# FFN entry and modulation loads: chains apart, own buffers, the factor between token halves, GpSimd's additions on VectorE

## The chip, the cores and the metric

The kernel runs on one core of a Trainium2 chip. The metric is the device time in microseconds of one execution, the median of three runs. TensorE (PE in the profile, with PEld for its weight loads), VectorE (DVE), ScalarE (ACT), GpSimd (POOL) and SyncE (SP, which issues the DMA of weights) work side by side, each through its own queue in order, and wait for each other by semaphores.

## The reference, cut to what matters

Two transformer blocks, each of two layers, run one after the other on 512 tokens of width 1024; the first block has 256 context tokens as well in its first layer.

```python
# first block, per layer: a modulation of six vectors from c (and from c_ctx)
mod_l = split(silu(c) @ ada_w[layer] + ada_b[layer], 6)
h_lat = rms(xl) * (1 + mod_l[1]) + mod_l[0]
y_lat = mixer(h_lat, ...)            # layer 0: conv + mLSTM scans; layer 1: latent attention (MLA)
xl = xl + mod_l[2] * y_lat
xl = xl + mod_l[5] * conv_ffn(rms(xl) * (1 + mod_l[4]) + mod_l[3])   # 1024 -> 2 x 2816 -> 1024
# second block, per layer
m = hybrid_mixer(rms_norm(x))        # differential attention, three dilated windows, rotary embedding
x = x + rms_norm(m)
x = x + rms_norm(swiglu(rms_norm(x)))
```

All is float32. The 12 MB matrix `ada_w[0]` is read for layer 0, and as much for layer 1.

## The kernel before, in words

Activations lie with the 1024 channels on partitions, in eight tiles (k = 0 to 7) of 128 channels by 512 tokens (768 with the context). A float32 product is made of three matmuls: each operand is split into a high part that the fast matmul format holds and a low remainder, and `staged`, `fm_g` and the helpers around line 366 issue high by high, high by low and low by high for each k. `weights` (L282) loads 512 KB of a weight matrix by SP's queue into a tile `raw`, ScalarE casts it to `whi` (L287), VectorE subtracts for `wlo` (L288). The pool `w` holds three buffers of each of the three tags.

The program runs through `first` (norm and first modulation), `mixer0` (convolution and mLSTM, 62 to 385 us, with its output projection to about 445 us), `conv_ffn` of layer 0 (to 1047 us), `mixer1a` and `mixer1b` (MLA, to 1450 us), `conv_ffn` of layer 1 (to 1835 us), then for each layer of the second block `mixer2` and `ffn2` (1835 to 2770 us, 2770 to 3746 us).

An FFN begins with `staged`: the weights of its first three column blocks stand ready, and three chains of 8 x 3 matmuls run over the eight k, k outermost, so that each new tile of the normed input (`h`, or `xg` in the second block) feeds three chains. In the FFNs with context that is done for the context, then for the latent tokens; elsewhere for the two halves of the tokens (`HALF`, 256 each). The normed input comes tile by tile from a loop on VectorE and ScalarE (`turn_loop`, `post_loop` with `pre_g`), and the sums of squares from `add_sq` (L460) and `pre_g` (L1487), with GpSimd adding the squares that ScalarE makes. The rms factor itself is made by `rstd` and `make_R`: TensorE sums over partitions (L434, L438), VectorE scales (L446), GpSimd takes the power -1/2 (L448, `rs_x`), TensorE broadcasts (L454). In the second block the factor R isn't applied to `xg` but to the products behind it, so it is wanted only with the first products; `mixer2` and `ffn2` call `make_R` before the first group of `staged`.

The modulation matrices are read by `ada` (L523): a generator that loads 512 KB through `raw`, so through the same three buffers as the weight matrices, and issues two matmul rows per load on a PSUM tile `ps_ad` (L536). It is drawn on by `side` and `fill` as side work amid the mLSTM (`more`), at the turn and in `conv_ffn` (two loads after each pair of hidden blocks). `rope` (L1533, second block) makes the rotary embedding: ScalarE copies the product out of PSUM, four DMAs swap halves (`rsw`), VectorE multiplies by the cosine (L1540), GpSimd by the sine (L1541), VectorE adds (L1546 or L1548).

The code gives what depends on what; a scheduler with its own estimates of durations sets the order on each engine from it, within the buffers of the pools. `pin` ties some instructions to a place relative to TensorE's work.

Of the kernel before, what the change touches and what calls it, by code (L numbers as in the profile page):

```python
# [14 lines left out]
AF = mybir.ActivationFunctionType  # L15
# [217 lines left out]
class Prog:  # L233
# [225 lines left out]
    def add_sq(self, S, k, src, a, tile):  # L459

        nc = self.nc
        n = src.shape[-1]
        q = S[0][:, a : a + n]
        if k == 0:
            nc.scalar.activation(q, src, AF.Square)
            return
        t = tile()[:, :n]
        nc.scalar.activation(t, src, AF.Square)  # L468
        if k < KD - 1:
            self.pin(nc.gpsimd.tensor_tensor(q, q, t, ALU.add))  # L470
        else:
            S[1] = t
# [53 lines left out]
    def ada(self, layer, ch):  # L526
# [137 lines left out]
    def staged(self, srcs, rhs, ctx=False, tag="mm"):  # L664

        mm = self.mm
        ws = [self.weights(s, lo=self.nc.vector) for s in srcs]

        def chains(ws, outs, a, b):
            for k in range(KD):  # L670
                xh, xl = (t[:, a:b] for t in rhs[k])
                for (wh, wl), o in zip(ws, outs):
                    w = slice(P * k, P * k + P)
                    mm(o, wh[:, w], xh, start=(k == 0), stop=False)
                    mm(o, wh[:, w], xl, start=False, stop=False)
# [12 lines left out]
        chains(ws, lat, TC, TA)  # L688
        return [list(q) for q in zip(lat, c)]
# [376 lines left out]
    def conv_ffn(self, layer, hs, ctx, begin, sq, loop=None):  # L1066
# [6 lines left out]
        with tc.tile_pool(name=f"f{layer}", bufs=1) as fp:  # L1073
# [7 lines left out]
            first = self.staged([up[i] for i in range(3)], hs, ctx)  # L1081
# [85 lines left out]
    def mixer1a(self, mp, hs):  # L1167
        nc, tc, I = self.nc, self.tc, self.I
        SEG = self.SEG
        if True:  # L1170
# [4 lines left out]
            with tc.tile_pool(name="m1t", bufs=2) as tp:  # L1175
# [6 lines left out]
                nc.gpsimd.tensor_tensor(acc, acc, s, ALU.add)  # L1182
# [37 lines left out]
                for k in range(4):  # L1220
# [3 lines left out]
                    else:  # L1224
                        s = self.tl(tp, [P, TA], "sqt")
                        nc.scalar.activation(s[:, :T], o, AF.Square)
                        if k < 3:
                            nc.gpsimd.tensor_tensor(acc[:, :T], acc[:, :T], s[:, :T], ALU.add)
# [101 lines left out]
    def mla_kv(self, tp, qd, ckv, rc, KR, krs, Ks, Vs):  # L1330
        nc = self.nc
        w = self.weights(self.I["m_ukv"][qd])
        for tb in range(6):
# [14 lines left out]
            nc.gpsimd.tensor_tensor(k[:, :, 0:64], k[:, :, 0:64], rk.unsqueeze(2).to_broadcast([P, 4, 64]), ALU.mult)  # L1348
            nc.gpsimd.tensor_tensor(
# [7 lines left out]
    def mla_q(self, tp, qd, cq, rq, tab, Qs, scs):  # L1357
        nc = self.nc
        ws = [self.weights(self.I["m_uq"][qd * 2 + i], 768) for i in range(2)]
        for tb in range(4):  # L1360
# [17 lines left out]
            for i, src in enumerate((r1, r2, r1, r2)):  # L1378
                nc.gpsimd.tensor_tensor(t[:, i], src, tab[:, i, tb].unsqueeze(1).to_broadcast([P, 4, 16]), ALU.mult)
# [110 lines left out]
    def pre_g(self, st, k, a, b):  # L1490
# [4 lines left out]
        if k == 0:  # L1495
            nc.scalar.activation(acc[:, a:b], x, AF.Square)
        else:
            s = sq()
            nc.scalar.activation(s[:, : b - a], x, AF.Square)
            self.pin(nc.gpsimd.tensor_tensor(acc[:, a:b], acc[:, a:b], s[:, : b - a], ALU.add))  # L1500
        return low

    def post_loop(self, ys, R, g, a, b, after):
# [3 lines left out]
        after_last = int(g == "ffn_post1")  # L1507
# [11 lines left out]
    XP = ((), (0, 2, 4, 6))  # L1519
# [10 lines left out]
    def rope(self, ap, ps, classes=False):  # L1530
# [10 lines left out]
        nc.gpsimd.tensor_tensor(sw, sw, self.SR, ALU.mult)  # L1541
# [11 lines left out]
    def mixer2(self, l, xg, acc, after):  # L1553
        nc, tc, I = self.nc, self.tc, self.I
        av = acc.rearrange("p (i b) -> p i b", b=4)
        R = self.make_R(acc)
        for k in range(KD):
            for t in xg[k]:
                tc.keep_in_program_order(nc.gpsimd.tensor_copy(t[:, T:TX], t[:, :64]))
        r = self.rstd(  # L1560
            [acc[:, i * P : i * P + P] for i in range(4)] + [av[:, :, b] for b in range(4)]
            + [[(0, acc[:, 448:]), (64, acc[:, :64])]] + [acc[:, t : t + P] for t in V0[1:]], D, EPS, "x12",
        )
        with tc.tile_pool(name=f"ma{l}", bufs=2) as ap:
            tab = ap.tile([P, 2, T], F32, name="rope2", bufs=1)
            nc.sync.dma_start(tab, I["rope2"])
            nc.vector.tensor_tensor(tab, tab, R.unsqueeze(1).to_broadcast([P, 2, T]), ALU.mult)
# [45 lines left out]
            for i, (o,) in enumerate(self.staged(srcs[:3], xg)):  # L1613
                dq[i // 2].append(rope(o))
# [80 lines left out]
    def merge(self, ap, l, gates, gts, of):  # L1695
# [10 lines left out]
        for d in range(KD):  # L1706
# [5 lines left out]
            nc.gpsimd.tensor_tensor(g[0], g[0], g[1], ALU.add)  # L1712
# [224 lines left out]
    def ffn2(self, l, xg, acc, nxt, after):  # L1937
        nc, tc, I = self.nc, self.tc, self.I
        R = self.make_R(acc)
        with tc.tile_pool(name=f"sf{l}", bufs=1) as fp, tc.tile_pool(name=f"st{l}", bufs=2) as tp:  # L1940
            ys = [fp.tile([P, T], F32, name=f"fy{k}") for k in range(KD)]
            acc, acc2 = (self.tl(tp, [P, T], "nacc", bufs=2) for _ in range(2))
            S = [acc, None]
# [37 lines left out]
            first = [o for (o,) in self.staged([I[f"sup{l}"][i] for i in range(3)], xg)]  # L1981
# [154 lines left out]
```

## Time and profile before

| | us |
|---|---|
| median of three runs | 3740.7 (3739.66 to 3743.14) |
| the profiled execution | 3747.83, span 3746.0 |
| TensorE busy in the span | 3625.1 (97%) |
| VectorE, ScalarE, GpSimd busy | 2154.5, 1417.7, 412.7 |
| TensorE's mean granted clock | 0.985 |

The clock is given as a share of full speed, 2.4 GHz; its other level is 0.5. Busy times are of the one profiled execution, and a row of the profile always names the line of the kernel that issued the instruction. Matmuls overlap each other, so the distance between two starts, and not the length of one, is what a matmul costs in a dense stretch.

### The profile page before, as it was taken

Reading aid. Unit: us, or ns where it says so; the run is one execution under the profiler, and the core shown is the slowest. Engines: PE = TensorE matmul, PEld = TensorE weight load, DVE = VectorE, ACT = ScalarE, POOL = GpSimd, SP = SyncE. Lnnn points to the kernel's source line nnn. Section 1 sums busy time; section 2 is a strip of 40 time slices with the busy share of each in tenths; the row PEclk is TensorE's granted clock in tenths of the full one; section 3 lists DMA queues with packets and bytes.
Section 4 is the critical chain, followed back from the end, with each engine's and each line's share of the span. In section 5 each row is a group of like instructions: output and inputs, shape, how many; then the busy total and the mean of one; then the engine's idle time right before and its main releaser. Section 6 shows DMA issues by size and latency. Waiting matters only on the chain. (4 is left out here: it accounts for less than half of the span.)

```text
span 3746.0 us, 50182 instructions
## 1 busy us (share of the span) xinstructions
PE 3625.1 (97%) x19870; PEld 2980.6 (80%) x19870; DVE 2154.5 (58%) x3568; ACT 1417.7 (38%) x2540; POOL 412.7 (11%) x460
## 2 busy tenths in 40 slices
PE   8999999999989999999999999999999999999998
PEld 5767777888876767888887888888888887888887
DVE  6958454444447676555575655645567655555545
ACT  3246232222236555333353333432235433333222
POOL 0000100000024211000201110300031111020001
PEclk9999999999999999999999999999999999999999
DMA  5242223331111011232333322233324333222332
GB/s 211 78 159 87 72 89 124 114 107 63 58 51 30 27 35 53 93 96 96 99 111 96 100 87 79 82 93 101 96 80 123 103 91 91 74 85 90 96 100 75
DMA packets 107387, 336.89 MB, mean 90 GB/s; under 512 B 14864, under 2 KB 19600, under 8 KB 106896
## 3 DMA queue, kind: packets, MB, share of 16 engines
q1 hardware_dynamic: 94864, 316.89, 26.6%
q10 hardware_dynamic: 12288, 16.79, 1.7%
q8 instruction: 156, 2.56, 0.3%
q14 instruction: 79, 0.65, 0.1%
HBM read 310.55 MB, written 2.10 MB: 83 GB/s over the span
## 5 line engine op out<-in xcount | busy, mean ns | idle before, releaser
L287 ACT CAST whi<-raw 128x1024 fp32r<-128x1024 f32 (+2 forms) x487 | 501.1, 1031 | 1201.1 <-PE ps_mm L367 764.7
L288 DVE TENSOR_TENSOR wlo<-raw,whi 128x1024 fp32r<-128x1024 f32 (+2 forms) x487 | 614.5, 1263 | 372.3 <-ACT whi L287 369.9
L367 PE MATMUL ps_mm<-h,whi 128*128 128x512 f32 (+1 forms) x2561 | 638.4, 356 | 7.7 <-DVE fy L1136 3.4
L367 PE MATMUL ps_mm<-xg,whi 128*128 128x512 f32 (+1 forms) x1865 | 554.5, 379 | 9.7 <-DVE xg L302 6.7
L367 PEld LDWEIGHTS ps_mm<-h,whi 128*128 128x128 f32 x2561 | 424.4, 189 | 94.9 <-issue 14.0
L367 PE MATMUL ps_mm<-hid,whi 128*128 128x512 f32 (+1 forms) x1805 | 469.3, 357 | 0.0
L367 PEld LDWEIGHTS ps_mm<-xg,whi 128*128 128x128 f32 x1865 | 346.5, 190 | 78.3 <-DVE xg L302 11.1
L366 PE MATMUL ps_mm<-xg,whi 128*128 128x512 f32 (+1 forms) x1271 | 390.3, 387 | 2.7 <-DVE xg L302 2.7
L367 PE MATMUL ps_mm<-h,wlo 128*128 128x512 f32 (+1 forms) x1282 | 391.3, 354 | 0.5 <-DVE wlo L288 0.5
L367 PEld LDWEIGHTS ps_mm<-hid,whi 128*128 128x128 f32 x1805 | 310.2, 188 | 59.5 <-issue 6.7
L367 PE MATMUL ps_mm<-xg,wlo 128*128 128x512 f32 (+1 forms) x934 | 350.7, 378 | 0.5 <-DVE wlo L288 0.5
L367 PE MATMUL ps_mm<-hid,wlo 128*128 128x512 f32 (+1 forms) x903 | 299.2, 356 | 0.0
L366 PEld LDWEIGHTS ps_mm<-xg,whi 128*128 128x128 f32 x1271 | 233.4, 190 | 48.7 <-DVE xg L302 4.3
L367 PEld LDWEIGHTS ps_mm<-h,wlo 128*128 128x128 f32 x1282 | 216.2, 190 | 37.2 <-DVE wlo L288 1.0
L366 PE MATMUL ps_mm<-xg,wlo 128*128 128x512 f32 (+1 forms) x634 | 240.6, 382 | 0.0
L367 PEld LDWEIGHTS ps_mm<-xg,wlo 128*128 128x128 f32 x934 | 177.7, 190 | 32.6 <-DVE wlo L288 1.0
L367 PEld LDWEIGHTS ps_mm<-hid,wlo 128*128 128x128 f32 x903 | 160.3, 188 | 24.9
L1541 POOL TENSOR_TENSOR rsw<-rsw,rope 128x512 f32<-128x512 f32 x64 | 109.6, 1714 | 465.4 <-DMA rsw<-rsw 285.7
L366 PEld LDWEIGHTS ps_mm<-xg,wlo 128*128 128x128 f32 x634 | 120.0, 189 | 23.0
L1160 DVE SCALAR_TENSOR_TENSOR xl<-ps_mm,mod,xl 128x512 f32<-128x512 f32 (+1 forms) x102 | 73.0, 717 | 109.4 <-PE ps_mm L367 108.7
L366 PE MATMUL ps_mm<-whi,xg 128*128 128x512 f32 x384 | 131.7, 411 | 1.9 <-ACT qk L1535 1.9
L829 DVE SCALAR_TENSOR_TENSOR acc<-up,cw,acc 128x783 f32<-128x783 f32 x120 | 120.6, 1027 | 1.2
(569 smaller groups left out, 5665.3 us busy)
## 6 DMA issues: line engine op xcount, KB each, us to landing
raw<-in_fup SPq DMA_DIRECT2D x88, 512.0 KB, 3.5
raw<-in_sup SPq DMA_DIRECT2D x88, 512.0 KB, 3.5
raw<-in_ada SPq DMA_DIRECT2D x80, 512.0 KB, 3.8
raw<-in_l_qk SPq DMA_DIRECT2D x48, 512.0 KB, 3.6
raw<-in_fdn SPq DMA_DIRECT2D x32, 512.0 KB, 3.5
raw<-in_d_v SPq DMA_DIRECT2D x32, 512.0 KB, 3.7
raw<-in_d_gt SPq DMA_DIRECT2D x32, 512.0 KB, 3.6
raw<-in_sdn SPq DMA_DIRECT2D x32, 512.0 KB, 3.4
```

The costliest lines, as they stand in the source:

```text
L287: self.nc.scalar.copy(h[:, :n], r[:, :n])
L288: (lo or self.nc.vector).tensor_tensor(l[:, :n], r[:, :n], h[:, :n].bitcast(F32), ALU.subtract)
L366: return self.nc.tensor.matmul(out, w, x, **k)
L367: return self.nc.tensor.matmul(out, w, x, **k)
L829: nc.vector.scalar_tensor_tensor(acc, u, s, acc, ALU.mult, ALU.add)
L1160: self.pin(nc.vector.scalar_tensor_tensor(xs, o[:, : b - a], self.m(layer, 5, d, int(a < TC)), xs, ALU.mult, ALU.add))
L1541: nc.gpsimd.tensor_tensor(sw, sw, self.SR, ALU.mult)
```

## The change

Five edits, each in several places:

1. `ada` loads into tiles `adaw` of its own, two buffers in the pool `ad`, instead of `raw`.
2. `staged` takes `apart`: for the last three k the loop goes chain by chain, not k by k. `conv_ffn` and `ffn2` call it with 3.
3. `staged` takes `between`, a function called between the two token halves; `mixer2` and `ffn2` make the prenorm factor there.
4. In `add_sq` and `pre_g` the addition of squares goes from GpSimd to VectorE and is issued one k later, so that VectorE doesn't wait for ScalarE's square.
5. Other elementwise operations go from GpSimd to VectorE: residual additions of the last post loop, the multiplications in `rope`, K, Q and norms of the MLA mixer, one gate sum in `mixer2`.

```diff
@@ add_sq
-        if k < KD - 1:
-            self.pin(nc.gpsimd.tensor_tensor(q, q, t, ALU.add))
-        else:
+        for u, v in S[2:]:
+            self.pin(nc.vector.tensor_tensor(u, u, v, ALU.add))
+        S[2:] = [(q, t)] if k < KD - 1 else []
+        if k == KD - 1:
             S[1] = t
@@ ada
-                r = self.raw(self.I[f"ada{layer}"][(ch + c if layer else ch + c - 4) * 4 + kg])
+                r = self.tl(self.adp, [P, WC], "adaw", bufs=2)
+                nc.sync.dma_start(r, self.I[f"ada{layer}"][(ch + c if layer else ch + c - 4) * 4 + kg])
@@ staged
-    def staged(self, srcs, rhs, ctx=False, tag="mm"):
+    def staged(self, srcs, rhs, ctx=False, tag="mm", apart=0, between=None):
...
         def chains(ws, outs, a, b):
-            for k in range(KD):
+            pairs = list(zip(ws, outs))
+            n = KD - apart
+            order = [(k, i) for k in range(n) for i in range(len(pairs))]
+            order += [(k, i) for i in range(len(pairs)) for k in range(n, KD)]
+            for k, i in order:
+                (wh, wl), o = pairs[i]
                 xh, xl = (t[:, a:b] for t in rhs[k])
-                for (wh, wl), o in zip(ws, outs):
-                    w = slice(P * k, P * k + P)
-                    mm(o, wh[:, w], xh, start=(k == 0), stop=False)
-                    mm(o, wh[:, w], xl, start=False, stop=False)
-                    mm(o, wl[:, w], xh, start=False, stop=(k == KD - 1))
+                w = slice(P * k, P * k + P)
+                mm(o, wh[:, w], xh, start=(k == 0), stop=False)
+                mm(o, wh[:, w], xl, start=False, stop=False)
+                mm(o, wl[:, w], xh, start=False, stop=(k == KD - 1))
...
             for a, b in self.HALF:
                 chains(ws, [o[:, a:b] for o in outs], a, b)
+                if between and a == 0:
+                    between()
@@ conv_ffn
-            first = self.staged([up[i] for i in range(3)], hs, ctx)
+            first = self.staged([up[i] for i in range(3)], hs, ctx, apart=3)
@@ pre_g
-        else:
-            s = sq()
-            nc.scalar.activation(s[:, : b - a], x, AF.Square)
-            self.pin(nc.gpsimd.tensor_tensor(acc[:, a:b], acc[:, a:b], s[:, : b - a], ALU.add))
-        return low
+            return low
+        s = sq()[:, : b - a]
+        nc.scalar.activation(s, x, AF.Square)
+
+        def rest():
+            self.pin(low())
+            return nc.vector.tensor_tensor(acc[:, a:b], acc[:, a:b], s, ALU.add)
+
+        return rest
@@ post_loop
-            self.pin((nc.gpsimd if k in self.XP[after_last] else nc.vector).tensor_tensor(x, x, y, ALU.add))
+            self.pin(nc.vector.tensor_tensor(x, x, y, ALU.add))
@@ rope
-        nc.gpsimd.tensor_tensor(sw, sw, self.SR, ALU.mult)
+        nc.vector.tensor_tensor(sw, sw, self.SR, ALU.mult)
@@ mixer2 (ffn2 likewise, with make_R alone and apart=3)
-        R = self.make_R(acc)
+        R = r = None
...
+            def factors():
+                nonlocal R, r
+                R = self.make_R(acc)
+                nc.vector.tensor_tensor(tab, tab, R.unsqueeze(1).to_broadcast([P, 2, T]), ALU.mult)
+                r = self.rstd(...)
...
-            for i, (o,) in enumerate(self.staged(srcs[:3], xg)):
+            for i, (o,) in enumerate(self.staged(srcs[:3], xg, between=factors)):
```

The same replacement of `nc.gpsimd` by `nc.vector` is made in `mixer1a`, `mixer1b`, the K and Q parts of MLA and the gate sum of `mixer2`.

How the orders differ at three places. On TensorE in the mLSTM's steps behind the second head: `xl` and `xc` are the scores' operands, `v,S` the products with the values, `cmu` and `g_T` belong to the convolution's norm. Before:

```order
L1039 MATMUL ps_ml_2591<-v_4_1673,S_414_2607 128x129
L1039 MATMUL ps_ml_2591<-v_5_1676,S_414_2607 128x129
L1003 MATMUL ps_ml_2680<-xl_915,xc_1262 128x128 x2
L1003 MATMUL ps_ml_2680<-xl_915,xl_1261 128x128 x2
L454 MATMUL ps_st_2508<-con,cmu_2506 128x128 x4
L454 MATMUL ps_st_2509<-con,cmu_2506 128x128 x2
L1003 MATMUL ps_ml_2681<-xl_915,xl_1261 128x128 x2
L1039 MATMUL ps_ml_2680<-v_0_1661,S_431_2688 128x129
L1039 MATMUL ps_ml_2680<-v_1_1664,S_431_2688 128x129
```

and now:

```order
L1047 MATMUL ps_ml_2591<-v_5_1676,S_414_2607 128x129
L1011 MATMUL ps_ml_2680<-xl_915,xc_1262 128x128 x2
L454 MATMUL ps_st_2508<-con,cmu_2506 128x128 x4
L454 MATMUL ps_st_2509<-con,cmu_2506 128x128 x2
L1011 MATMUL ps_ml_2680<-xl_915,xl_1261 128x128 x2
L1011 MATMUL ps_ml_2681<-xl_915,xl_1261 128x128 x2
L538 MATMUL ps_ad_2707<-adaw_4479,sc 32x512 x2
L538 MATMUL ps_ad_2707<-adaw_4483,sc 32x512 x2
L454 MATMUL ps_st_2641<-con_593,g_T_696 128x128 x4
L548 MATMUL ps_ad_4489<-con,adarow_4487 128x8 x4
L454 MATMUL ps_st_2642<-con_593,g_T_696 128x128 x2
```

The matmuls of two modulation loads (`adaw`) stand now between the scores and the convolution's norm, where before there was none in such a step.

On TensorE at the first group of the conv FFN of layer 0, `ps_mm_3956`, `3957` and `3958` are the three chains, `4135` the fourth, which takes the PSUM buffer that the first pair's work leaves free. Before, the end of the three chains:

```order
L367 MATMUL ps_mm_3956<-h_3315,whi_3938 128x512
L367 MATMUL ps_mm_3956<-h_3316,whi_3938 128x512
L367 MATMUL ps_mm_3956<-h_3315,wlo_3939 128x512
L367 MATMUL ps_mm_3957<-h_3315,whi_3944 128x512
L367 MATMUL ps_mm_3957<-h_3316,whi_3944 128x512
L367 MATMUL ps_mm_3957<-h_3315,wlo_3945 128x512
L367 MATMUL ps_mm_3958<-h_3315,whi_3950 128x512
L367 MATMUL ps_mm_3958<-h_3316,whi_3950 128x512
L367 MATMUL ps_mm_3958<-h_3315,wlo_3951 128x512
L367 MATMUL ps_mm_4135<-h_3301,whi_4131 128x512
```

and now:

```order
L367 MATMUL ps_mm_3958<-h_3314,whi_3950 128x512
L367 MATMUL ps_mm_3958<-h_3313,wlo_3951 128x512
L367 MATMUL ps_mm_3958<-h_3315,whi_3950 128x512
L367 MATMUL ps_mm_3958<-h_3316,whi_3950 128x512
L367 MATMUL ps_mm_3958<-h_3315,wlo_3951 128x512
L538 MATMUL ps_ad_5555<-adaw_6390,sc 32x512 x2
L538 MATMUL ps_ad_5555<-adaw_6456,sc 32x512 x2
L367 MATMUL ps_mm_4135<-h_3301,whi_4131 128x512
```

The last nine matmuls of each chain stand together now (of the third the last five are shown), and the matmuls of two modulation loads stand ahead of the fourth chain.

On VectorE in the differential attention of the second block, `p` are the probabilities, `drs` their factors, `rope` the tables. Before:

```order
L1846 TENSOR_SCALAR p_16091<-p_16091,drs_16093 128x512
L1540 TENSOR_TENSOR qk_16134<-qk_16134,rope_15374 128x512
L1847 SCALAR_TENSOR_TENSOR p_16086<-p_16086,drs_16093,p_16091 128x512
L288 TENSOR_TENSOR wlo_16325<-raw_16322,whi_16324 128x1024
L1838 TENSOR_REDUCE mx_16184<-ps_st_16178 128x1
L446 TENSOR_SCALAR rv_d_2971_16172<-dss_15809 128x4
L1548 TENSOR_TENSOR qk_16134<-qk_16134,rsw_16136 128x512
```

and now, in such a unit:

```order
L1861 TENSOR_SCALAR p_16621<-p_16621,drs_16623 128x512
L1550 TENSOR_TENSOR rsw_16691<-rsw_16691,rope_15340 128x512
L1551 TENSOR_TENSOR rsw_16693<-rsw_16693,rope_15340 128x512
L1862 SCALAR_TENSOR_TENSOR p_16616<-p_16616,drs_16623,p_16621 128x512
L1556 TENSOR_TENSOR qk_16690<-rsw_16691,rsw_16693 128x512
```

The multiplication by the sine (L1551) stands in VectorE's queue, where it stood in GpSimd's.

## Rows read from the trace of the kernel before

**Rows 1.** page, busy time of each engine, share of the span, number of instructions

```profile
PE 3625.1 (97%) x19870; PEld 2980.6 (80%) x19870; DVE 2154.5 (58%) x3568; ACT 1417.7 (38%) x2540; POOL 412.7 (11%) x460
```

**Rows 2.** stretches: length, then PE, PEld, DVE, ACT, POOL busy (x), PEclk, DMA share, GB/s

```profile
319.00:361.00 42.00, 36.55 (x245) 32.87 (x244) 35.60 (x100) 32.32 (x100) 2.64 (x2) 0.88 0.08 23
...
443.00:460.00 17.00, 12.30 (x77) 9.47 (x78) 4.84 (x10) 2.32 (x5) 1.74 (x2) 0.80 0.45 147
479.00:490.00 11.00, 7.64 (x27) 5.86 (x26) 9.71 (x13) 6.51 (x9) 0.00 (x0) 0.84 0.47 143
490.00:1047.00 557.00, 554.18 (x3183) 465.46 (x3181) 259.52 (x366) 154.61 (x193) 13.66 (x12) 1.00 0.29 92
```

**Rows 3.** two of the stretches, line L536 (modulation matmuls) alone: PE, PEld, PEclk, DMA share, GB/s

```profile
319.00:361.00 42.00, 0.00 (x0) 0.00 (x0) 0.88 0.08 23
490.00:1047.00 557.00, 23.96 (x144) 3.66 (x144) 1.00 0.29 92
```

**Rows 4.** waits of PE: engine, tile, line <- releaser: us in total, times, longest us

```profile
PE ps_st L1854 <- DVE p L1847: 7.7, 4, 3.0
...
PE ps_ad L536 <- DMA raw<-in_ada: 6.9, 5, 3.9
PE ps_mm L367 <- DVE xg L302: 6.7, 19, 1.6
PE ps_st L454 <- POOL rs_x L448: 5.7, 5, 1.4
...
PE ps_st L434 <- POOL p L470: 1.6, 1, 1.6
...
PE ps_st L434 <- POOL GB L470: 1.4, 1, 1.4
```

**Rows 5.** groups by line and shape, GpSimd: xcount | busy us, mean ns | idle

```profile
L1541 POOL TENSOR_TENSOR rsw<-rsw,rope 128x512 f32<-128x512 f32 x64 | 109.6, 1714 | 465.4 <-DMA rsw<-rsw 285.7 <-DMA rsw<-qk 147.9 <-PE ps_mm L367 14.7
```

**Rows 6.** page, DMA issues: xcount, KB each, median us from issue to landing

```profile
raw<-in_ada SPq DMA_DIRECT2D x80, 512.0 KB, 3.8
```

**Rows 7.** timeline at the turn: start us, us, engine, line, tiles, count, idle before

```profile
442.41 0.80 SPq L279 DMA_DIRECT2D raw<-in_ada  x2
...
448.08 3.19 PE L536 MATMUL ps_ad<-raw,sc 128*32 128x512 f32 x8 [3.92 <-DMA raw<-in_ada]
```

**Rows 8.** timeline at the conv FFN's first pair

```profile
473.98 0.39 PE L367 MATMUL ps_mm<-h,wlo 128*128 128x512 f32 x1
...
474.20 0.62 PE L367 MATMUL ps_mm<-h,whi 128*128 128x512 f32 x2
...
482.28 0.74 DVE L1136 SCALAR_TENSOR_TENSOR fy<-ps_mm,par,fy 128x511 f32<-128x511 f32 x1
...
483.17 0.70 PE L367 MATMUL ps_mm<-h,whi 128*128 128x512 f32 x2 [3.36 <-DVE fy L1136]
```

**Rows 9.** timeline in the post loop at an entry, VectorE and GpSimd

```profile
2409.40 0.48 DVE L302 SCALAR_TENSOR_TENSOR xg<-xl,par,xg 128x256 fp32r<-128x256 f32 x1
...
2410.30 0.42 DVE L1511 TENSOR_TENSOR xl<-xl,v 128x256 f32<-128x256 f32 x1
...
2410.41 0.91 POOL L1500 TENSOR_TENSOR rsw<-rsw,p 128x256 f32<-128x256 f32 x1 [2.06 <-ACT p L1499]
...
2410.65 0.96 DVE L302 SCALAR_TENSOR_TENSOR xg<-xl,par,xg 128x256 fp32r<-128x256 f32 x1
```

**Rows 10.** timeline in the differential attention, VectorE and GpSimd

```profile
2019.67 0.49 DVE L1846 TENSOR_SCALAR p<-p,drs 128x512 f32<-128x512 f32 x1
...
2033.16 0.69 DVE L1540 TENSOR_TENSOR rsw<-rsw,rope 128x512 f32<-128x512 f32 x1 [0.89 <-DMA rsw<-rsw]
2033.29 1.68 POOL L1541 TENSOR_TENSOR rsw<-rsw,rope 128x512 f32<-128x512 f32 x1 [6.38 <-DMA rsw<-rsw]
2033.77 1.49 DVE L1846 TENSOR_SCALAR p<-p,drs 128x512 f32<-128x512 f32 x1
...
2036.57 1.11 PE L1854 MATMUL ps_st<-con,p 128*128 128x128 f32 x4 [2.99 <-DVE p L1847]
```

More of the change, by code (lines that the diff above doesn't have):

```diff
@@ L1181, in mixer1a @@
                         self.split(ckv[k][0][:, a:b], ckv[k][1][:, a:b], o[:, : b - a], scale=self.par("kv_norm", k, k + 1))
-                nc.gpsimd.tensor_tensor(acc, acc, s, ALU.add)
+                nc.vector.tensor_tensor(acc, acc, s, ALU.add)
                 rc = self.rstd([acc[:, i * P : i * P + P] for i in range(6)], 256, EPS, "rc")
@@ L1227, in mixer1a @@
                         if k < 3:
-                            nc.gpsimd.tensor_tensor(acc[:, :T], acc[:, :T], s[:, :T], ALU.add)
+                            nc.vector.tensor_tensor(acc[:, :T], acc[:, :T], s[:, :T], ALU.add)
                     self.split(cq[k][0], cq[k][1], o, scale=self.par("q_norm", k, k + 1))
@@ L1347, in mla_kv @@
             rk = self.rstd_of(ss, 4, 96, EPS, "k4")
-            nc.gpsimd.tensor_tensor(k[:, :, 0:64], k[:, :, 0:64], rk.unsqueeze(2).to_broadcast([P, 4, 64]), ALU.mult)
-            nc.gpsimd.tensor_tensor(
+            nc.vector.tensor_tensor(k[:, :, 0:64], k[:, :, 0:64], rk.unsqueeze(2).to_broadcast([P, 4, 64]), ALU.mult)
+            nc.vector.tensor_tensor(
                 k[:, :, 64:96], KR[:, tb].unsqueeze(1).to_broadcast([P, 4, 32]),
@@ L1378, in mla_q @@
             for i, src in enumerate((r1, r2, r1, r2)):
-                nc.gpsimd.tensor_tensor(t[:, i], src, tab[:, i, tb].unsqueeze(1).to_broadcast([P, 4, 16]), ALU.mult)
+                nc.vector.tensor_tensor(t[:, i], src, tab[:, i, tb].unsqueeze(1).to_broadcast([P, 4, 16]), ALU.mult)
             nc.vector.tensor_tensor(r1, t[:, 0], t[:, 1], ALU.subtract)
@@ L1517, in post_loop @@
             self.pin(low())
-    XP = ((), (0, 2, 4, 6))
     def make_R(self, acc):
@@ L1559, in mixer2 @@
                 tc.keep_in_program_order(nc.gpsimd.tensor_copy(t[:, T:TX], t[:, :64]))
[L1560 to L1563, printed above, removed]
         with tc.tile_pool(name=f"ma{l}", bufs=2) as ap:
@@ L1566, in mixer2 @@
             nc.sync.dma_start(tab, I["rope2"])
-            nc.vector.tensor_tensor(tab, tab, R.unsqueeze(1).to_broadcast([P, 2, T]), ALU.mult)
+            def factors():
+                nonlocal R, r
+                R = self.make_R(acc)
+                nc.vector.tensor_tensor(tab, tab, R.unsqueeze(1).to_broadcast([P, 2, T]), ALU.mult)
+                r = self.rstd(
+                    [acc[:, i * P : i * P + P] for i in range(4)] + [av[:, :, b] for b in range(4)]
+                    + [[(0, acc[:, 448:]), (64, acc[:, :64])]] + [acc[:, t : t + P] for t in V0[1:]], D, EPS, "x12",
+                )
             self.CR, self.SR = tab[:, 0], tab[:, 1]
@@ L1711, in merge @@
                 nc.vector.scalar_tensor_tensor(g[i], g[i], 1.0, q, ALU.add, ALU.mult)
-            nc.gpsimd.tensor_tensor(g[0], g[0], g[1], ALU.add)
+            nc.vector.tensor_tensor(g[0], g[0], g[1], ALU.add)
             hl = [self.tl(ap, [P, T], "od", F32R, bufs=4) if d < 4 else rest[:, d - 4], lows[d // 4][:, d % 4]]
@@ L1938, in ffn2, with factors @@
         nc, tc, I = self.nc, self.tc, self.I
-        R = self.make_R(acc)
+        R = None
         with tc.tile_pool(name=f"sf{l}", bufs=1) as fp, tc.tile_pool(name=f"st{l}", bufs=2) as tp:
             ys = [fp.tile([P, T], F32, name=f"fy{k}") for k in range(KD)]
-            acc, acc2 = (self.tl(tp, [P, T], "nacc", bufs=2) for _ in range(2))
-            S = [acc, None]
+            sums, acc2 = (self.tl(tp, [P, T], "nacc", bufs=2) for _ in range(2))
+            S = [sums, None]
+            def factors():
+                nonlocal R
+                R = self.make_R(acc)
             def hidden(g, u):
@@ L1980, in ffn2 @@
             pend = None
-            first = [o for (o,) in self.staged([I[f"sup{l}"][i] for i in range(3)], xg)]
+            first = [o for (o,) in self.staged([I[f"sup{l}"][i] for i in range(3)], xg, apart=3, between=factors)]
             first.append(up(3))
```

1 line of the change is left out of this document (removed).

## The prediction

> **What bounds the kernel now.** First the page's busy times: TensorE is busy for 97% of the span, VectorE for 58%, ScalarE for 38%, GpSimd for 11% [rows 1]. So the time is TensorE's own work plus the moments in which it stands or runs at the lower clock, and an edit on another engine counts only where it ends such a moment. Work that is moved from one place of TensorE's queue to another is not saved; it is saved only as far as it falls into idle time there.
>
> Next the table of stretches, which says where that idle time is [rows 2]. In the first conv FFN (490 to 1047 us) TensorE is busy for 554.18 of 557 us at full clock: whatever leaves that stretch shortens it one to one. In the last part of the mLSTM (319 to 361 us) it is busy for 36.55 of 42 us, and the granted clock is 0.88 in the mean, a mixture of 2.4 GHz and 1.2 GHz: 5.45 us idle and, at 12% of 42 us, some 5.0 us lost to the clock, together about 10.5 us that other work could fill. At the turn from the mixer to the FFN (443 to 460 us) 4.7 of 17 us are idle and the clock is 0.80; at the FFN's first pair (479 to 490 us) 3.36 of 11 us, at 0.84.
>
> Then the waits of TensorE, which name who ends them [rows 4]: the modulation weights' DMA (6.9 us in five waits), VectorE's prenorm chunks (6.7 us in 19), the attention's p (7.7 us in four), GpSimd's rs_x (5.7 us in five), and GpSimd's sums of squares at the turns (1.6 and 1.4 us). Together under one percent of the span; this is the field on which the change plays, and no edit of it can bring much more than 1%.
>
> **Own buffers for the modulation weights.** There are 80 loads of 512 KB, each used by two matmul rows. Before, they take turns with the weight matrices in three buffers; now they have two of their own, and nothing but their own use holds them back. In the order the loads then stand earlier. Counted by place (before the mLSTM; mLSTM up to 319 us; its rest; turn; conv FFN) there were 11, 29, 0, 4 and 36; now there are 19, 25, 22.5, 10.5 and 3 (a half is a load whose two rows are apart). The price of one: the 36 loads in the conv FFN are 144 records of 23.96 us [rows 3], so 0.67 us each.
>
> The sum by places. Out of the dense conv FFN go 33 x 0.67 = 22.0 us, in full. Eight more before the mLSTM, where TensorE is dense too, cost 5.3 us; four fewer up to 319 us give 2.7 us; 6.5 more at the turn cost 4.3 us. That is +6.9 us. Left are 22.5 loads in the 42 us from 319 us on, where there were none [rows 3]: 15.0 us of work. If everything idle there is filled, the stretch grows by 15.0 - 10.5 = 4.5 us, and the whole edit gives -22.0 + 6.9 + 4.5 = -10.6 us. But with two buffers a load can be issued only when the load before the last has been used, so two loads pass in one landing plus one use. The median landing is 3.8 us [rows 6], so the pace is (3.8 + 0.67) / 2 = 2.2 us a load, 22.5 x 2.2 = 50 us, a growth of 8 us. So the edit gives **-7 us**. The far end is the landing of a crowded moment: two loads issued together at 442.41 us were awaited until 448.08 us, 5.6 us [rows 7]. At that landing the pace is 3.1 us, the stretch 70.5 us, and the edit +13.4 us. It is even where the stretch becomes 57 us, at a landing of 4.4 us. I take the median since little else is loaded from 319 us on: the DMA share there is 0.08 [rows 2].
>
> The Trainium skill ("Trainium Kernel Development and Optimization", Best Practices) advises to double-buffer so that DMA and compute overlap. By that alone the 22.5 loads would cost no wait and the edit would be at its -10.6 us; the rows of the trace allow it only if a landing is below the time between two uses, which here is about the same.
>
> At the turn itself the wait of 3.92 us for the DMA [rows 7] doesn't simply go: five loads now stand there in a row, of which two buffers can hold two. The others are issued as the first are used, and land after the FFN's first h chunks are ready anyway. I take 0, between -3.9 and +4 (one more such wait).
>
> **The last three h tiles chain by chain.** In the conv FFN's first group three chains of 24 matmuls ran abreast, and the first ended six matmuls before the last. Now its end comes 18 matmuls before the last one's, 12 earlier. These matmuls start 0.23 us apart (473.98, 474.20 us, [rows 8]), so ScalarE's and VectorE's work on the first pair, whose last part starts at 482.28 us, can start 2.7 us earlier. In the new order two loads' matmuls (1.3 us, already counted) also stand ahead of the fourth chain. Together 4.0 us, against the wait of 3.36 us for fy [rows 8]: it goes, and with it most of the lower clock in that stretch, 16% of 11 us, 1.8 us. **-5 us**, with 0 as the other end (the ScalarE cast ahead of the first pair's work starts when weights come free, which may not move). At the two FFNs behind the second kind of mixer the same edit does little: there the order differs from that of before in only a few rows, since the chunks come late and the matmuls were already taken as they became ready.
>
> **The prenorm factor between the halves.** In the order its TensorE rows (the sum, the broadcast over rs_x) stand where they stood, behind the first matmuls of the next chain, at all three places but one, and there it is late in both. The 5.7 us of waits on rs_x remain. **0**, from -2.8 (half of them) to +1.4 (one more).
>
> **GpSimd's additions on VectorE.** GpSimd loses 286 rows, VectorE gains 283. Unhindered, a 128x256 addition takes 0.42 us on VectorE (2410.30 us, [rows 9]), where GpSimd took 0.91 us for it. The 64 multiplications of the rotary embedding took 1.71 us each on GpSimd [rows 5]; VectorE's sister operation of the same shape takes 0.69 us (2033.16 us, [rows 10]). VectorE gets more work, but also loses delays: beside the GpSimd addition of 2410.41 us its L302 took 0.96 us, against 0.48 us at 2409.40 us with GpSimd at rest [rows 9]; beside the GpSimd multiplication of 2033.29 us its L1846 took 1.49 us, against 0.49 us at 2019.67 us [rows 10]. In the loops that pace the entries one addition of 0.42 us per chunk stands against this relief (0.48 us for L302; I count it for every second chunk, and half as much for the other operations): about even, so the 6.7 us of waits on xg stay. What gets shorter are chains that end in such an operation: the waits on GpSimd sums (3.0 us, [rows 4]) lose the difference of 0.5 to 1 us each, and the attention's wait of 2.99 us at 2036.57 us sits behind the delayed L1846 and loses the 1.0 us of delay but gains the 0.69 us of the multiplication, which now stands on VectorE ahead of L1847's successor. I take **-3 us**; the far ends are -8 us (all of the sums' waits, and half of the attention's) and +8 us (VectorE's additional rows in the entry loops uncompensated: five entries of 8 chunks at 0.42 us make 16.8 us, half of it on the path). At the very end of the kernel four additions per half move from GpSimd to VectorE; the loop's pace there is one multiplication and one addition a chunk on either side: 0.
>
> On this the Trainium skill has a rule ("SBUF — State Buffer", Who interferes with whom): the two engines share a port pair, whoever starts first keeps it for the whole instruction, and a VectorE instruction with two SBUF inputs is blocked by a GpSimd one that reads. The rows fit: L1846 of 2033.77 us ends just after GpSimd does (2033.29 + 1.68 = 2034.97 us). By the rule in full, every moved operation frees VectorE of more than it costs, and this part would be at its -8 us. The skill also says ("Perfetto Trace Analysis", Optimizing Scalar/DVE Operations) that a saturated VectorE may gain from giving work to GpSimd, which speaks against the change; at 58% it isn't saturated.
>
> **The sum.** -7 - 5 - 3 = -15 us against the profiled execution's span of 3746.0 us, 3731 us. That run took 3747.8 us, 7.1 us above the median of 3740.7 us; the same 15 us off the median give **3726 us**. A measurement of this kernel can tell about 0.2%, 7.5 us, from no change.
>
> **Rivals.** *More is hidden (3712 us, -28.5):* all idle time in the mLSTM is filled (-10.6), the five DMA waits for modulation weights vanish (-6.9), the entry gives -5 and VectorE's relief -6. For it: DMA share 0.08 from 319 us on; against it: two buffers are fewer than three. *It doesn't do what it says (3737 us, -4):* a landing near 4.4 us makes the moved loads cost in the mLSTM what they save in the FFN, two of the titles (chains apart at three of four entries, factor between the halves) leave the order where it was, VectorE's gain and load cancel; only the 3.4 us at the first pair go. For it: the order itself shows this for those places. *Slower (3750 us, +9.4):* the two buffers set the pace. If a load lands 5.6 us after its issue, as at the turn, the mLSTM's end is paced by its 22.5 loads at 3.1 us: +13.4 us, +4 us for the second wait in the row of five at the turn, -8 us for the rest. It decides from a landing of 4.4 us on, and the total passes zero at about 5 us. For it: five loads in a row with two buffers; against it: the idle DMA queues there.
>
> **How the numbers follow.** Forecast (-8 to -23 us) 0.53; more hidden 0.11; no effect 0.25; slower 0.11. Faster by over 0.2% is the first two, 0.64; within 0.2% 0.25; slower 0.11. The range goes from 3710 us, which takes in most of "more hidden", to 3747 us, which takes in "no effect" and the milder half of what lies above: about 0.85 of the cases.
>
> **What would show it.** Right: no modulation matmuls in the conv FFN after its entry, that stretch some 22 us shorter, the mLSTM's end some 8 us longer with a clock near 1.0; no wait of TensorE on fy at the entry and no lower clock there; L302 in the post loops near 0.5 us, never 0.96 us. Wrong: waits on the modulation weights' DMA summing to well over 7 us, above all between 319 and 375 us (then the buffers pace it); a gap before the fourth chain still there; more waits on xg than 10 us (then VectorE has become the pace of the entries).

## The result, and the profile after

The changed kernel takes 3711.9 us in the median of four runs (3711.23 to 3715.2) beside 3741.9 us for the kernel before: a ratio of 0.9921, with an interval of 0.9904 to 0.9938, or 30 us less. Measured again beside three of the experiments it gave 0.9935 (0.9923 to 0.9947), 24 us less. The prediction was 15 us less, with a range of 3710 to 3747 us. The direction holds, and the range by 2 us; the gain is 1.6 to 2 times the forecast, and, as the experiments show, most of what is missing is one term.

The waits of TensorE after, answering to [rows 4] (engine, tile, line <- releaser: us in total, times, longest):

```profile
...
PE ps_ad L538 <- DMA adaw<-in_ada: 12.8, 10, 3.6
PE ps_st L1869 <- DVE p L1862: 7.0, 3, 3.5
PE two L367 <- DVE xl L1168: 6.5, 1, 6.5
PE ps_st L454 <- POOL rs_x L448: 5.8, 5, 1.4
PE ps_mm L367 <- DVE xg L302: 5.7, 17, 1.3
```

The row left out above these is one wait at the kernel's start, 15.2 us (16.7 us before), which no edit aims at. The waits for the modulation weights' DMA have nearly doubled (6.9 us before); 4.6 us of them lie between 319 and 375 us. The wait for fy is gone, those for rs_x stand where they stood, and of the attention's two lines one is left. The other, before, was

```profile
PE ps_st L1834 <- ACT p L1862: 7.1, 2, 4.3
```

and has shrunk to 0.3 us. The stretches, answering to [rows 2] and [rows 3], first all work and then line L538 alone (PE, PEld, DVE, ACT, POOL; then PE, PEld; PEclk, DMA share, GB/s):

```profile
319.00:361.00 42.00, 37.27 (x263) 26.11 (x260) 27.09 (x76) 27.37 (x87) 2.64 (x2) 1.00 0.55 183
443.00:475.00 32.00, 26.34 (x129) 16.76 (x127) 13.40 (x25) 8.79 (x14) 1.01 (x1) 0.84 0.44 148
475.00:490.00 15.00, 15.00 (x83) 11.49 (x84) 12.88 (x26) 6.29 (x9) 0.00 (x0) 1.00 0.33 106
490.00:1037.00 547.00, 543.35 (x3097) 472.75 (x3096) 271.10 (x386) 160.34 (x200) 0.70 (x1) 1.00 0.20 64
```

```profile
319.00:361.00 42.00, 11.13 (x52) 1.47 (x48) 1.00 0.55 183
490.00:1037.00 547.00, 2.12 (x12) 0.30 (x12) 1.00 0.20 64
```

The moved loads' matmuls are seen at the mLSTM's end, where there were none, and the clock there is now at full speed (0.88 before). The conv FFN holds 12 of their records in place of 144.

Where the two programs drift apart was read by pairing each instruction of one trace with its counterpart in the other. In the profiled executions the changed kernel is 9 us behind at 385 us, 17 us behind at 460 us (the moved loads), 10.8 us ahead at 825 us (the conv FFN gets 28 us shorter). It stays there until 1825 us, gains 12 to 14 us in the first mixer of the second block, loses 1 us in its FFN, gains 10 us in the second mixer and 2 us at the end. These are single executions. So about a third of the gain is the first block's, and two thirds are the second block's mixers, where the forecast had next to nothing.

### The profile page after: what moved, and what is told of

Read it like the earlier page. It is cut to its first block, busy times and chain, and to the rows that moved or that the text cites. A ratio compares the mean times of both kernels' runs of the same rounds, so it can differ in the third digit from the quotient of the medians.

```text
span 3709.8 us, 49898 instructions
## 1 busy us (share of the span) xinstructions
PE 3615.3 (97%) x19870; PEld 2973.6 (80%) x19870; DVE 2197.0 (59%) x3900; ACT 1418.6 (38%) x2540; POOL 98.2 (3%) x128
## 5 line engine op out<-in xcount | busy, mean ns | idle before, releaser
L288 DVE TENSOR_TENSOR wlo<-raw,whi 128x1024 fp32r<-128x1024 f32 (+2 forms) x487 | 582.4, 1197 | 396.4 <-ACT whi L287 393.1
L1984 DVE TENSOR_TENSOR fy<-ps_mm,fy 128x512 f32<-128x512 f32 (+1 forms) x92 | 57.0, 619 | 79.0 <-PE ps_mm L367 77.7
```

Of the source, the lines that this page charges most:

```text
L288: (lo or self.nc.vector).tensor_tensor(l[:, :n], r[:, :n], h[:, :n].bitcast(F32), ALU.subtract)
L1984: self.pin(nc.vector.tensor_tensor(y, o, y, ALU.add))
```

## The experiments

All were measured against the kernel before on the same chip. First one edit at a time, then the edits back and forth, then the open questions.

**Only the own buffers.** Edit:

```diff
-                r = self.raw(self.I[f"ada{layer}"][(ch + c if layer else ch + c - 4) * 4 + kg])
+                r = self.tl(self.adp, [P, WC], "adaw", bufs=2)
+                nc.sync.dma_start(r, self.I[f"ada{layer}"][(ch + c if layer else ch + c - 4) * 4 + kg])
```

> The kernel before with one edit: the modulation loads get their two own buffers. Theory A (the forecast's step): -7 us against before, from -10.6 (all idle time of the mLSTM's end filled) to +13 (the two buffers set the pace). The trace of the changed kernel shows the program 10.8 us earlier than before from 825 us on, with both this edit and the chains apart in it, and 12.8 us of waits for these loads. Theory B: the loads' waits eat the gain, and most of the 10.8 us belongs to the chains: then -3 us or less here. Expected by A: 3732 to 3737 us beside a before of 3741; by B: 3738 to 3742.

Measured: 0.9999 (0.9987 to 1.0012), nothing. Yet its trace shows the mechanism whole: 17 us behind at 500 us, 9.8 us ahead at 825 us. Of that 3.9 us are given back up to 1040 us, where each matmul is a little slower, and 3.8 us at the next turn, where the granted clock is lower (0.83 in the mean of 1030 to 1070 us, 0.91 before). At its end this one trace is still 7.5 us ahead; but the profiled execution of the kernel before was 7.1 us above its median, and over all executions nothing is left. The pace can be read from the starts of two six-matmul groups (a row names the first of its forms only). With the buffers alone:

```profile
900.03 0.51 PE L367 MATMUL ps_mm<-hid,wlo 128*128 128x512 f32 x2
900.38 0.87 PE L367 MATMUL ps_mm<-hid,whi 128*128 128x512 f32 x4
901.10 0.40 PE L367 MATMUL ps_mm<-hid,wlo 128*128 128x512 f32 x1
```

and with the buffers and the chains apart:

```profile
899.89 0.86 PE L367 MATMUL ps_mm<-hid,whi 128*128 128x512 f32 x4
900.58 0.51 PE L367 MATMUL ps_mm<-hid,wlo 128*128 128x512 f32 x2
900.93 0.51 PE L367 MATMUL ps_mm<-h,whi 128*128 128x512 f32 x2
```

Six matmuls, three of 512 and three of 256 columns, take 1.07 us in the one and 1.04 us in the other, with no wait between them. From 825 to 1040 us the run with both edits loses nothing by the pairing, the run with the buffers alone the 3.9 us. Why the pace differs I don't know; it is the one or the other for a whole stretch.

**Only the chains apart** (`apart=3` in `conv_ffn` and `ffn2`).

> The kernel before with one edit: the last three h tiles chain by chain, in both conv FFNs and both FFNs of the second block. Forecast: -5 us, all of it at the first pair of the conv FFN of layer 0 (the wait of 3.36 us for fy and the lower clock behind it), nothing at the other three. Rival: the ScalarE cast ahead of the first pair's work doesn't move and the wait stays: 0 us. A second rival: at the second block's FFNs it shortens the way to the first hidden block as well, -2 us more each, since the changed kernel's ffn2 stretches came out 0.9 and 2.4 us shorter: then -7 to -9 us.

Measured: 0.9989 (0.9974 to 1.0004), 4 us, not clear of nothing. In its trace the program is 2.3 us behind the kernel before at 460 us and 1.8 us ahead at 500 us: 4.1 us gained at this entry. At the first pair the wait shrank from 3.36 us to 0.89 us. VectorE's last step there starts at nearly the same time as before (482.12 against 482.28 us), which in a program that is 2.3 us late is 2.5 us earlier against the chains, and TensorE is released by another engine:

```profile
480.31 0.74 DVE L1139 SCALAR_TENSOR_TENSOR fy<-ps_mm,par,fy 128x511 f32<-128x511 f32 x1
481.93 1.04 ACT L287 CAST whi<-raw 128x1024 fp32r<-128x1024 f32 x1 [0.98 <-PE ps_mm L367]
482.12 0.74 DVE L1140 SCALAR_TENSOR_TENSOR fy<-ps_mm,par,fy 128x511 f32<-128x511 f32 x1
483.01 0.70 PE L367 MATMUL ps_mm<-h,whi 128*128 128x512 f32 x2 [0.89 <-ACT whi L287]
```

What follows: the forecast's step holds, and the rival of the expectation in part. The first pair's work is earlier with the end of the first chain, but the cast of the next weights comes late, and the fourth chain needs it. In the changed kernel the matmuls of two loads stand ahead of it, and no wait is left there.

**Only GpSimd's work on VectorE** (all that the change moves, the sums deferred by one k).

> The kernel before with one edit: all of GpSimd's additions and multiplications on VectorE, with the addition of squares issued one k later. Forecast: -3 us. The trace of the changed kernel speaks for more: between 1825 and 2250 us and between 2825 and 3175 us (the two mixers of the second block) it gains 12 and 10 us. Theory A: that comes from this edit, the rotary multiplication above all: -20 to -25 us. Theory B: it comes from the other edits (the factor between the halves, which lets the mixers' first chains go on), and this edit alone gives -3 us. Theory C: VectorE's additional rows cost at the entries: 0 or above.

Measured: 0.9961 (0.9946 to 0.9977), 15 us. Theory A holds in kind, as the next runs show for the rotary multiplication; its number was read from one pair of traces and is too high.

**Only the factor between the halves.**

> The kernel before with one edit: the prenorm factor made between the two token halves in the mixers and FFNs of the second block. Forecast: 0 us (within 2), since the TensorE rows of the factor stand where they stood. Rival (theory B of the VectorE run): the mixers' gain of 12 and 10 us comes from here: -15 us or more.

Measured: 1.0004 (0.9992 to 1.0016), nothing. The rival falls.

**Only the rotary multiplication.** Edit:

```diff
-        nc.gpsimd.tensor_tensor(sw, sw, self.SR, ALU.mult)
+        nc.vector.tensor_tensor(sw, sw, self.SR, ALU.mult)
```

> The kernel before with one operation moved: the rotary multiplication by the sine on VectorE, all other GpSimd work stays. Theory A: the gain of the VectorE run (-13 us, two thirds of it in the two differential mixers) is the rotary chain, freed of 1.7 us on GpSimd and of the delays that GpSimd lays on VectorE: -9 to -13 us here, and the waits behind p of the attention (4.28 and 2.99 us at 2032 and 2037 us before) lose some 4 us in each mixer. Theory B: the gain comes from the sums and additions: 0 to -4 us here.

Measured: 0.9958 (0.9943 to 0.9972), 16 us: all that VectorE's edit gives, from 64 of the 332 instructions that the pages show moved (VectorE 3568 before, 3900 after). Its profiled execution was the fastest of eleven, 8 us below their median, so its rows flatter it a little. The attention's two waits (7.7 us behind VectorE's p, 7.1 us behind ScalarE's, before) became:

```profile
PE ps_st L1854 <- DVE p L1847: 9.0, 3, 3.5
...
PE ps_st L1834 <- ACT p L1862: 0.6, 1, 0.6
```

**The changed kernel with the rotary multiplication back on GpSimd.**

> The changed kernel with the rotary multiplication back on GpSimd. Theory A: it loses 9 to 13 us of the 30: some 20 us faster than before remain (3721 us). Theory B: it stays near the changed kernel, 3712 to 3716 us. It also tells whether the parts add up: the sum of the four single edits was some -17 us, the whole -30.

Measured: 0.9974 (0.9959 to 0.9988), 10 us faster than before. Against the changed kernel's 0.9935 that is 15 us lost (20 us against its first 0.9921), more than the 9 to 13 us expected, and the rotary edit's 16 us from the other side.

**Own buffers and chains apart together.**

> The kernel before with the two edits of the first block's FFN together: own buffers for the modulation weights, and chains apart. Alone they gave 0 and -4 us (each within 5). In the changed kernel's trace the program stood 10.8 us earlier behind both. Theory A: they help each other: the loads' matmuls stand ahead of the fourth chain and the down projections don't get the slower pace (236 ns a matmul in place of 230 ns between 860 and 1030 us) that the run with the buffers alone showed: -8 to -12 us. Theory B: they add: -4 us, and the rest of the 10.8 us in the trace comes from the additions on VectorE.

Measured: 0.9968 (0.9954 to 0.9981), 12 us, as theory A said. That the two edits help each other isn't shown: alone they gave 0 and 4 us, and the 8 us between are no more than the uncertainty of such a difference. At 825 us, behind the first pair, this trace is 8.5 us ahead of before, the one with the buffers alone 9.8 us; what differs is the slower pace behind it, which isn't there. Together with the rotary edit's 15 to 16 us this is the whole change: some 27 us, where two measurements gave 24 and 30 us. The remaining edits (the other additions, the factor) are worth 0 within what can be measured.

**Three own buffers** (`bufs=3` in the changed kernel).

> The changed kernel with three own buffers for the modulation weights in place of two. The prediction's slower rival said that two buffers pace the moved loads; in the changed kernel TensorE waits 12.8 us in ten waits for them, 5.7 us of it at 459 and 464 us with 10 us at the lower clock behind. Theory A: the buffers' number is the cause: the waits fall to 5 us or less and the kernel gains 5 to 10 us (3702 to 3707 us). Theory B: the landing itself sets the wait (the loads stand too close together in the order whatever the number): 0 us, within 3.

Measured: 0.9944 (0.9922 to 0.9965), 21 us, no better than two. The waits for the loads fell as theory A said, but another wait stands in their place:

```profile
PE ps_mm L367 <- DVE xl L783: 6.4, 1, 6.4
...
PE ps_ad L538 <- DMA adaw<-in_ada: 2.2, 5, 0.8
```

With three buffers all loads are used before the turn, and there TensorE waits for VectorE's residual addition (xl) instead. With two it waits, at the same place, for the loads. The changed kernel at the turn (start us, us, engine, line, tiles, count, idle before):

```profile
454.32 1.06 PE L538 MATMUL ps_ad<-adaw,sc 128*32 128x512 f32 x8
...
455.42 5.21 SPq L534 DMA_DIRECT2D adaw<-in_ada  x3
458.97 3.18 PE L538 MATMUL ps_ad<-adaw,sc 128*32 128x512 f32 x8 [3.58 <-DMA adaw<-in_ada]
...
464.23 1.92 PE L538 MATMUL ps_ad<-adaw,sc 128*32 128x512 f32 x4 [2.08 <-DMA adaw<-in_ada]
466.08 0.80 PE L367 MATMUL ps_mm<-h,whi 128*128 128x256 f32 x2
```

The row of five loads does what the order promised, two at once and then a landing for the next ones; but of the 5.7 us waited there most would be waited anyway.

**The changed kernel again.**

> The changed kernel once more, on the same chip and against the same runs of the kernel before as the three beside it, since some 10 us between two chips' sessions decide the comparisons here. All theories: -25 to -31 us, ratio 0.9917 to 0.9933.

Measured: 0.9935 (0.9923 to 0.9947), 24 us, a little short of the 25 to 31 us expected.

**The broadcast really moved.** Edit to the changed kernel (`mixer2` likewise; `mm` keeps its last instruction in `self.newest`):

```diff
         r = self.rstd([acc[:, i * P : i * P + P] for i in range(4)], D, EPS, "x4")
+        meanwhile()
         Rp = self.ps("st")
-        self.over([r[:, i : i + 1] for i in range(4)], Rp)
+        with self.tc.issue_after(self.newest.ins):
+            self.over([r[:, i : i + 1] for i in range(4)], Rp)
...
-                R = self.make_R(acc)
+                R = self.make_R(acc, lambda: (next(fourth), next(fourth)))
...
-            first = [o for (o,) in self.staged([I[f"sup{l}"][i] for i in range(3)], xg, apart=3, between=factors)]
-            first.append(up(3))
+            first = [o for (o,) in self.staged([I[f"sup{l}"][i] for i in range(3)], xg, apart=3)]
+            fourth = self.fmk_g(I[f"sup{l}"][3], xg, [(0, T)], every=2)
+            factors()
+            first.append(self.whole(fourth)[0])
```

> The changed kernel with the prenorm factor's broadcast really moved: TensorE issues it only after 12 matmuls of the fourth chain (before and in the changed kernel two stand between the sum and it, where TensorE waits 1.39 us for rs_x at 2400, 2776 and 3349 us). Theory A: the three waits go, and the lower clock of 10 us behind the one at 2776 us shortens: -4 to -8 us against the changed kernel. Theory B: the sums, one column each, are what lowers the clock, and the later broadcast keeps the first rotary and gate operations waiting on VectorE: 0, or up to 3 us slower.

Measured: 0.9885 (0.9872 to 0.9898), 43 us faster than before and 19 us faster than the changed kernel beside it (0.9935): the best of all. Its waits:

```profile
PE ps_st L1933 <- DVE p L1926: 2.8, 5, 0.8
...
PE ps_st L456 <- POOL rs_x L450: 1.3, 2, 1.1
```

The waits on rs_x fell from 5.8 to 1.3 us, as theory A said. That and a shorter lower clock behind the wait at 2776 us (0.83 in the mean of 2770 to 2800 us in the changed kernel beside it, 0.89 here) would make theory A's 4 to 8 us; the measured 19 us is more than either theory allowed. Most of the rest lies in the attention, whose one row of waits for p (7.0 and 9.8 us in the changed kernel's two traces) isn't there any more; four smaller rows are left there, 3.5 us together. The edit makes part of the fourth projection ahead of the rotary embeddings, and the order of what fills the attention's gaps is another. That this order is the cause is argued from the traces, not tried by itself.

**GpSimd busy again, but on no chain.** Edit to the kernel with the rotary multiplication alone:

```diff
+        idle = self.tl(ap, [P, T], "echo", bufs=1)
+        nc.gpsimd.tensor_tensor(idle, out, self.SR, ALU.mult)
```

> The kernel before with the rotary multiplication on VectorE, and a multiplication of the same size given back to GpSimd behind each rotary embedding, whose result nothing reads: GpSimd works as long as before and beside the same VectorE work, but stands on no chain. (It does more work than the reference needs.) Theory A (the chain): what the rotary edit gained, some 15 us, came from the 1.7 us on GpSimd within the chain of each embedding: -10 us or more remain. Theory B (the shared port): it came from the delays that GpSimd lays on VectorE's instructions: 0 to -5 us remain.

Measured: 0.9998 (0.9988 to 1.0008): the whole gain is gone. GpSimd's 64 idle multiplications, VectorE's step on p beside them, and TensorE's waits:

```profile
L1550 POOL TENSOR_TENSOR echo<-qk,rope 128x512 f32<-128x512 f32 x64 | 104.8, 1637 | 469.9 <-DVE qk L1546 267.8 <-DVE qk L1548 139.5 <-DVE rsm L1905 21.4
```

```profile
L1848 DVE TENSOR_SCALAR p<-p,drs 128x512 f32<-128x512 f32 x32 | 16.6, 519 | 1.0
```

```profile
PE ps_st L1856 <- DVE p L1849: 7.6, 4, 3.6
PE ps_st L1856 <- DVE mx L1841: 4.2, 1, 4.2
...
PE ps_st L1836 <- ACT p L1864: 1.2, 1, 1.2
```

The three waits of 13.0 us are near those before (14.8 us) and not near the 9.6 us of the rotary edit. VectorE is busy for 2159.3 us with the rotary edit and for 2189.8 us here, with the same 3632 instructions. By the time, then, it is theory B: not the 1.7 us within the chain, but GpSimd's work beside VectorE's is what cost the time. The traces bear that out in one mixer only. The two mixers of the second block, cut by the pairing so that a mixer's rows hold the same work of TensorE (columns as for [rows 2]), in the kernel before, with the rotary edit, and with the idle multiplications behind it:

```profile
1825.00:2250.00 425.00, 411.71 (x2487) 347.33 (x2486) 253.94 (x452) 177.94 (x353) 66.32 (x56) 0.98 0.34 99
2760.00:3250.00 490.00, 472.20 (x2842) 399.62 (x2842) 308.88 (x551) 215.06 (x424) 88.83 (x78) 0.96 0.31 92
```

```profile
1817.70:2232.30 414.60, 408.15 (x2487) 346.14 (x2486) 257.06 (x484) 179.03 (x353) 12.09 (x24) 0.99 0.35 101
2743.20:3222.00 478.80, 466.67 (x2843) 396.09 (x2842) 310.07 (x583) 215.42 (x424) 33.31 (x46) 0.97 0.32 94
```

```profile
1826.60:2248.90 422.30, 411.51 (x2488) 348.01 (x2487) 270.32 (x484) 179.34 (x353) 64.34 (x56) 0.98 0.34 99
2762.20:3242.60 480.40, 465.87 (x2842) 394.80 (x2842) 326.46 (x583) 216.21 (x424) 85.77 (x78) 0.98 0.32 94
```

In the first mixer TensorE's matmuls stand in the rotary edit's order, and 7.7 of the 10.4 us gained are lost again: there GpSimd's work beside VectorE's is what costs the time, with the chain as short as in the rotary edit. In the second VectorE's busy time grows as much (16 us, 13 us in the first), but of the 11.2 us gained only 1.6 us are lost; TensorE's order there is neither that before nor the rotary edit's. So in the second mixer the cause stays open, and these are single executions. The idle instruction also keeps the embedding's buffer longer, but no wait in the trace ends with it.

**The modulation weights back in the shared buffers.**

> The changed kernel with the modulation weights back in the three shared buffers. Alone the own buffers gave 0, together with the chains apart -12 us where the chains alone gave -4. Theory A (they help each other): without them the changed kernel loses 8 to 12 us (3720 to 3724 us). Theory B (they add nothing): 3712 to 3716 us.

Measured: 0.9944 (0.9932 to 0.9957), 21 us. Against 0.9935 the own buffers are worth 3 us there; between the theories, and not clear of nothing.

## Why the prediction was right, and where it was wrong

*Bound.* Right: TensorE is at 97% in both. Its idle time in the span went from 120.9 to 94.5 us and its busy time, for the same 19870 matmuls, from 3625.1 to 3615.3 us at a mean granted clock of 0.989 in place of 0.985. The remark that no edit can bring much more than 1% also held: the whole change came to 0.65 to 0.8%.

*Own buffers (-7 us).* The mechanism is right: loads out of the conv FFN, into the mLSTM's end, which now runs at full clock. The sum by places was off at both ends. From 500 to 825 us the FFN gets 26 us shorter and not 22 us: a load's two rows cost 0.8 us there, by the distance of starts, and not the 0.67 us of busy time that I took from [rows 3]. Against that the program is 17 us behind when it comes to the FFN, where the sum's terms make 15 us. What it is worth is not well measured: alone 0, in the changed kernel 3 us, beside the chains apart 8 us, each with some 5 to 8 us either way; the 7 us lie within that spread. The sign of being wrong that I had named, waits for these loads well over 7 us, did show: 12.8 us, so the buffers do pace the loads, and the edit still didn't cost time. At the turn I expected a wait that doesn't simply go, and so it is.

*Chains apart (-5 us).* The mechanism is right: the first pair's work came 2.5 us earlier against the chains (2.7 us forecast), and the entry gains 4.1 us in the trace of this edit alone. By the medians it is 4 us, not clear of nothing. The end I named for it, a cast that comes late, is what still holds TensorE for 0.89 us there; in the changed kernel no wait is left, with the matmuls of two loads ahead of the fourth chain.

*The factor between the halves (0 us).* Right: the scheduler left it where it was. The run in which the broadcast was really held back shows what it was worth.

*GpSimd's additions on VectorE (-3 us).* This is the step that failed, by 12 us: the runs gave 15 us for all of it and 16 us for the rotary multiplication alone. (The pages count 332 instructions that change engines, not 286 and 283.) I priced two things, the entry loops, where relief and addition cancel (right: the waits on xg went from 6.7 to 5.7 us), and a single wait of the attention, where "1.0 us of delay" went against "0.69 us of the multiplication". What I left out is that this happens at 64 embeddings amid 32 attention steps: the term was sized from one place, and the far end of -8 us had only half of the attention's waits. The relief per instruction differs. Before, L302 and the step on p took

```profile
L302 DVE SCALAR_TENSOR_TENSOR xg<-xl,par,xg 128x256 fp32r<-128x256 f32 x60 | 40.8, 687 | 0.9 <-ACT xg L301 0.9
...
L1846 DVE TENSOR_SCALAR p<-p,drs 128x512 f32<-128x512 f32 x32 | 17.6, 548 | 1.0
```

and after, they have the durations of the unhindered ones:

```profile
L302 DVE SCALAR_TENSOR_TENSOR xg<-xl,par,xg 128x256 fp32r<-128x256 f32 x60 | 28.6, 478 | 0.0
...
L1861 DVE TENSOR_SCALAR p<-p,drs 128x512 f32<-128x512 f32 x32 | 15.6, 486 | 1.0
```

The large relief, of L302, bought next to nothing, since the rotary edit alone, which leaves L302 at 683 ns, gains as much; the step on p took 519 ns in the run with the idle multiplications. By the rule of the Trainium skill ("SBUF — State Buffer", Who interferes with whom) I had put this part at -8 us, nearer than my -3 us and still only half of what was measured. The run with the idle multiplications agrees with it as far as VectorE is concerned: beside GpSimd's work the same instructions take 30 us longer in all, even where nothing waits for its result. The single row that I set beside the rule was a poor witness: L1846 has one tensor input, and the rule as I told it is about two. Instructions with two show it as well: L288, which subtracts for wlo, took 1292 ns in the mean before, 1261 ns with the rotary edit and 1284 ns with the idle multiplications.

*Rivals.* "More is hidden" (3712 us) hit the number, largely by luck: the mLSTM's gaps were filled, but the DMA waits grew from 6.9 to 12.8 us instead of vanishing, and VectorE's relief, put at 6 us, was 15 us. That the range held, whose near end was set for this rival, is owed to the same luck. "Slower" fell: the two buffers do pace the loads at the turn, but in front of a wait that is there anyway; three buffers show it.

## What to carry to other kernels

Before counting a wait as a cost, ask what is late next at that place: here a third buffer took away 10 us of waits and gained nothing that could be measured. Don't take work on GpSimd beside a busy VectorE for free because no one waits for it: here 64 such instructions undid 16 us, and their price should have been summed over all the places where they run, not read at one. Look for a broadcast or reduction that the scheduler put right behind its slow factor: holding it back by a dozen matmuls took away 4.5 us of waits here, in an edit that gained 19 us.

## What the hardware showed that I had not expected

The lower clock behind one and the same wait lasts differently long. TensorE stands 5.7 to 6.5 us ahead of the second mixer of the first block in every run. The granted clock of the stretch from 1030 to 1070 us is 0.91 in the kernel before, 0.96 with the rotary edit alone, 0.79 with three buffers, and, for the changed kernel itself, in its two profiled executions:

```profile
1030.00:1070.00 40.00, 33.12 (x208) 25.25 (x207) 25.76 (x42) 17.22 (x28) 1.01 (x1) 0.91 0.15 46
```

```profile
1030.00:1070.00 40.00, 33.12 (x184) 26.77 (x186) 22.65 (x38) 14.60 (x23) 1.01 (x1) 0.83 0.09 27
```

The program is the same in both, and from 0.91 to 0.83 is 3.2 us of such a stretch. Single traces therefore differ by several microseconds that belong to no edit, which is why the worth of each edit rests on the medians, and why the shares by stretch, which come from pairs of traces, are rough. The other surprise is the pace of dense matmuls shown with the first experiment, 1.04 or 1.07 us for the same six.
